# Retention's latent pass: element-wise sums moved from GpSimd to VectorE, and later adaLN products

## The chip, the cores and the metric

The kernel runs on one core of a Trainium2 chip. Five engines share the work and run side by side, each taking its own instructions strictly in order: TensorE (PE: matmuls and transposes), VectorE (DVE), ScalarE (ACT), GpSimd (POOL) and SyncE (SP, which here issues most of the loads). They wait for each other through semaphores. The metric is device time in microseconds (us) of one launch.

## The reference, cut to what matters

Two layers over 512 latent tokens and 256 context tokens of width 1024, all in float32. The first layer mixes tokens by neighbourhood attention and spatial gating, the second by retention; each ends with a gated MLP. The change lies in the second layer's mixer, with eight heads of 128 key columns and 256 value columns:

```python
q, k, v, g = jnp.split(h_lat @ w_in, splits, axis=-1)
q = apply_rope(q.reshape(B, T, H, dk), cos, sin)
k = apply_rope(k.reshape(B, T, H, dk) * dk ** -0.5, cos, sin)
for d in range(2):                       # forward and backward over the tokens
    s_ctx = retention_final_state(rev(kc), rev(vc), lg)
    outs_lat.append(rev(retention_chunked(rev(q), rev(k), rev(v), lg, s_ctx)))
y_lat = retention_output(outs_lat[0] + outs_lat[1], g, gn_g, w_out)

def apply_rope(x, cos, sin):
    x1, x2 = jnp.split(x, 2, axis=-1)
    return jnp.concatenate([x1 * c - x2 * s, x1 * s + x2 * c], axis=-1)
```

So each head needs keys, queries, values and gates of all latent tokens, two decay matrices, and the state that the context tokens leave behind. Beside this, every layer takes shift, scale and gate vectors ("adaLN") from a product of SiLU(c) with a 1024 x 6144 matrix.

## The kernel before, in words

A float32 product is made of three fast products: every operand is split into a high part (ACT writes it) and a low part (DVE writes the difference), and `mm3` adds high x high, high x low and low x high. `split` stands behind every weight and every activation that a matmul reads, so each loaded 128x1024 weight tile costs one ACT and one DVE instruction.

Retention runs in two passes. The **context pass** goes over the eight heads and makes each one's context state: weights `rck`, `rcv`, products into `rkc` and `rvc`, states `stc` (written to memory as `rsd`). In the same loop the adaLN products for later stages are slipped in, one step of a job at a time, by `self.bg(...)`: a step loads two 512 KB tiles (`ar`) on SP's queue and runs four matmuls `ad`, a later step copies the sum (`mr`) and adds the bias row by a DMA that POOL issues, and for a gate a last one makes the product `ag`. The weight tiles of the heads and the `ar` tiles share three buffers named `raw`.

The **latent pass** goes over the heads again. The keys and queries of a head, and then its values and gates, are one 2x2 block product that is worked by a seven-product scheme in the manner of Strassen: instead of eight products there are seven, whose operands are sums of blocks. On the weight side the function `sums` makes four such sums per product, three by GpSimd and one by VectorE, each followed by a split: `a1`, `a2` (weights as loaded), `s2`, `q3`, `q4`, `s3` (sums), `b2`. In the trace the weights of a head h are `rwk`/`rwq` (128x512 halves, for keys and queries) and `rwa1`, `rwa2`, `rwb1`, `rwb2` (128x1024, for values and gates), their split forms `rkq..` and `rvg..`; the products go to the PSUM tiles `Xkq`, `Ykq`, `Zkq` and `Xvg`, `Yvg`, `Zvg`. The results gather in `kp` and `qp` (keys, queries) and `vp`, `rv`, `rg` (values, gates). `rope` turns `kp` and `qp`: ACT copies swapped halves to `sw`, GpSimd multiplies them with `sin`, VectorE multiplies the tile with `cos` and adds both. `decay` makes the decay matrix of a head from two exponentials (`e`): a product and a sum with the identity, both on GpSimd.

`kq_product` calls `after(n)` behind each of its seven products, and `vg_product` likewise; the main loop's `in_kq` and `in_vg` put other work there: the next weights' steps (`step`), the decay, the transposes of the previous head's output (`gated`, tiles `rt`), and one eighth of the previous head's output projection (`o()`: six matmuls `w`, an ACT copy `ryp` and a DMA `yr` that POOL issues). The one wait that the text below speaks of most is that of the seventh product `Xkq<-sar`: it writes PSUM tile X again, so it must wait until DVE's instruction `qp<-qp,Xkq` has read the sixth product from it.

What the program code says is not quite the order on the engines: a scheduler, with an own account of costs, sets each engine's order from the program and its dependencies.

All engine operations pass through one helper, so nearly every instruction of the trace has its line, 64 (63 after the change).

Of the kernel before, what the change touches and what calls it, by code (L numbers as in the profile page):

```python
# [13 lines left out]
ALU = mybir.AluOpType  # L14
# [15 lines left out]
NEG = -1e30  # L30
RB = 32
GF = 2
CTX_BG = 1
ND = 389
EARLY = 2
TWO = ((0, (0, 1), 0, True), (1, (2,), 0, False), (1, (3,), 128, True))
# [35 lines left out]
class Trunk:  # L72
# [1098 lines left out]
    def retention(self, y, final):  # L1171
        S, V, T, G, a = self.S, self.V, self.T, self.G, self.a
        KS = float(np.float32(P) ** np.float32(-0.5))
        with ExitStack() as ctx:
# [6 lines left out]
            sin = rp.tile([P, 512], F32, name="sin", tag="sin")  # L1181
# [31 lines left out]
            def ctx_keys(h):  # L1213
                ps = self.ps(f"rkc{h}", "A")
                self.proj_t(ps[:, :256], hd[h]["wk"], 1)
                if h:
                    kc = rp.tile([P, 256], F32, name=f"kc{h}", tag=("pre0", "pre1")[h % 2], bufs=1)
                else:
                    kc = self.t2k("kc0", shape=(P, 256))
                hd[h]["kc"] = kc  # L1220
                S.activation(kc, ps[:, :256], AF.Copy, scale=KS)
# [65 lines left out]

            def sums(a1, a2, b1, b2, put, both=None):

                add = lambda o, x, y: G.tensor_tensor(out=o, in0=x, in1=y, op=ALU.add)  # L1290
                if both:
                    put("a1", both)
                else:
                    put("a1", a1)
                    yield
                    put("a2", a2)
                add(a1, a1, b1)
                add(b1, b1, b2)
                yield
                put("s2", b1)  # L1300
                V.tensor_tensor(out=b1, in0=a1, in1=b2, op=ALU.add)
                add(a2, a2, b1)
                yield
                put("q3", b1)
                yield
                put("q4", a2)
                yield
                put("s3", a1)
                yield
                put("b2", b2)  # L1310
                yield
# [73 lines left out]
            def decay(h):  # L1385
                d = hd[h]
                e = d["e"] = []
                for i in range(2):
                    t = rp.tile([P, ND], F32, name=f"e{i}{h}", tag=f"e{i}", bufs=1)
                    lg = dec[:, 8 * i + h : 8 * i + h + 1]  # L1390
                    S.activation(t, dist[:, i * ND : i * ND + ND], AF.Exp, scale=lg)
                    e.append(t)
                dl = d["dl"] = e[0][:, 0:384]
                G.tensor_tensor(out=dl, in0=dl, in1=e[1][:, 0:384], op=ALU.mult)
                G.tensor_tensor(out=dl[:, 128:256], in0=dl[:, 128:256], in1=self.ident, op=ALU.add)

            def rope(x, dst, scale, name):

                sw = self.t2k(f"sw{name}")

                def one():
                    for o, i in ((slice(0, 64), slice(64, 128)), (slice(64, 128), slice(0, 64))):
                        S.activation(sw[o], x[i], AF.Copy, scale=scale)
                    G.tensor_tensor(out=sw, in0=sw, in1=sin, op=ALU.mult)
                    V.scalar_tensor_tensor(out=x, in0=x, scalar=scale, in1=cos, op0=ALU.mult, op1=ALU.mult)

                def two():
                    V.tensor_tensor(out=x, in0=x, in1=sw, op=ALU.add)
                    self.split(dst[0], dst[1], x)

                return one, two
# [239 lines left out]
            for h in range(8):  # L1651
                ctx_keys(h)
                if h == 1:
                    self.need(1)
                if h:
                    ctx_states(h - 1)
                ctx_values(h)
                if h < 7:
                    ctx_weights(h + 1)
                else:  # L1660
                    kq = kq_weights(0)
                    next(kq)
                    next(kq)
                if h == 0:
                    self.need(0)
                elif h < 5:
                    next(blocks, None)
                if h == 5:
                    self.load(cos, a["cos"])
                    self.load(sin, a["sin"])  # L1670
                    self.load(gng, a["gn_col"])
                if h == 6:
                    vg = vg_weights(0)
                self.bg(CTX_BG)
            ctx_states(7)
            for _ in kq:
                pass
            out = []

            def o():  # L1680
                if out:
                    out.pop(0)()
# [8 lines left out]
            def step(x):  # L1691
                if x:
                    next(x, None)

            for h in range(8):
                d = hd[h]
                f, later = [], None

                def in_kq(n):
                    if n == 0:  # L1700
                        o()
                        if h in (0, 6, 7):
                            step(vg)
                    elif n == 1:
                        o()
                        if 0 < h < 6:
                            wo.append(w_out(h - 1))
                    elif n == 2:
                        o()
                        decay(h)  # L1710
                    elif n == 3:
                        o()
                        step(vg)
                    elif n == 4:
                        step(vg)
                    elif n == 5:
                        if h:
                            f.extend(gated(h - 1))
                            if h < 6:
                                out.extend(out_steps(h - 1, f, list(wo)))  # L1720
                            else:
                                feats.extend(f)
                    elif n == 6:
                        step(vg)

                def in_vg(n):
                    nonlocal later
                    if n == 0:
                        step(vg)
                        self.bg()  # L1730
                    elif n == 1:
                        step(vg)
                    elif n == 2:
                        step(vg)
                        context(h)
                        self.bg()
                        if h < 7:
                            later = kq_weights(h + 1)
                    elif n == 3:
                        step(vg)  # L1740
                        score(h, 0)
                    elif n == 4:
                        self.bg()
                    elif n == 5:
                        score(h, 1)
                        states(h)
                        within(h, 0)
                        step(later)

                kq_product(h, in_kq)  # L1750
                vg_product(h, in_vg, o)
                if h == 7:
                    self.bg_all()
                    flat = lambda b: [self.blk[b].rearrange("p x k c -> p x (k c)")[:, x] for x in range(2)]
                    at = [flat(("t", 1)), flat(("t", 2)), flat(22), self.at_slot(3, "rwo3"), flat(("t", 3)), self.at_slot(0, "rwo5")]
                    ws = [self.unit(row(10 + i), f"rwo{i}", at[i]) for i in range(4)]
                    for t in toks:
                        y[t] = self.ytile(t, "yr")
                        self.load(y[t], yd[t])
                    sums_ = {(t, n): self.ps(f"wr{t}{n}", "A") for t in toks[:2] for n in range(2)}  # L1760

                    def part(t, n, fs):
                        c, o = self.gcol(t), slice(512 * n, 512 * n + 512)
                        for i in fs:
                            self.mm3(sums_[t, n], [x[:, c] for x in feats[i]], [x[:, o] for x in ws[i]], i == 0, i == 5)
                step(later)
                step(later)
                within(h, 1)
                step(later)
                step(later)  # L1770
                step(later)
                if h < 7:
                    vg = vg_weights(h + 1)
                if h < 5:
                    wo[:] = []
                    wo.append(w_out(h))
                across(h, 0)
                across(h, 1)
                across(h, 2)
                across(h, 3)  # L1780
                norm(h)
# [7 lines left out]
            for t in toks:  # L1789
                for n in range(2):  # L1790
# [3 lines left out]
                    o = slice(512 * n, 512 * n + 512)  # L1794
# [523 lines left out]
```

## Time and profile before

| | |
|---|---|
| median of 3 runs | 1889.61 us (1889.36 to 1892.18) |
| the profiled execution's own time | 1894.07 us |
| its span, first to last instruction | 1892.3 us |
| busy, share of the span | PE 94%, DVE 75%, ACT 59%, POOL 24% |
| context pass of retention, about | 905 to 1044 us of the span |
| latent pass of retention, about | 1044 to 1480 us of the span |
| latent pass alone: PE, DVE, ACT, POOL busy | 406.9, 360.7, 264.8, 184.7 of 436 us |

Matmuls overlap each other, so a PE that is busy is not one at its peak; what can be read directly is where PE sits idle and who ended the wait. An instruction's time is from its start to its end, stalls while it runs included. In the rows, `out<-in` names the tiles written and read, `x8` counts instructions, and `<-` behind an idle time names who ended it.

### The profile page before, as it was taken

The numbers are of one execution on the slowest core, as the hardware profiler recorded it, in microseconds if no ns is written. First come the engines' busy times: TensorE is split into PE (matmuls) and PEld (weight loads), VectorE is DVE, ScalarE is ACT, GpSimd is POOL, SyncE is SP. The second block draws the span as 40 slices with busy tenths as digits, with TensorE's granted clock in tenths as the row PEclk, the third lists the DMA queues.
The fourth block names the chain that finished last, engine by engine and source line by source line (L and its number), as shares of the span: only waits on it lengthen the run. The fifth ranks groups of instructions, "written<-read, shape, count | busy, mean of one in ns | idle before, by whom it ended". The sixth has DMA issues, their size and how long they took to land. (4 is left out here: it accounts for less than half of the span.)

```text
span 1892.3 us, 29833 instructions
## 1 busy us (share of the span) xinstructions
PE 1785.2 (94%) x11240; PEld 1587.8 (84%) x11240; DVE 1424.1 (75%) x2349; ACT 1114.6 (59%) x2038; POOL 454.3 (24%) x533
## 2 busy tenths in 40 slices
PE   6999999999999999998999899999998989999998
PEld 4887677889889899898778788888898789899987
DVE  4543567579787887778876778778889689788887
ACT  4533567466555655555575556666666477576664
POOL 1111211100222222221211334434543100222221
PEclk9999999999999999999999999999999989999999
DMA  7432332324687776776576343665433324777773
GB/s 303 134 103 87 115 106 68 122 80 145 162 184 178 156 164 139 171 149 166 213 228 220 121 150 116 152 163 128 103 93 106 123 91 145 179 199 178 174 182 103
DMA packets 95488, 279.21 MB, mean 148 GB/s; under 512 B 12528, under 2 KB 14064, under 8 KB 95344
## 3 DMA queue, kind: packets, MB, share of 16 engines
q1 hardware_dynamic: 63568, 217.88, 35.2%
q0 software_dynamic: 31200, 59.31, 18.6%
q8 instruction: 88, 1.44, 0.3%
q14 instruction: 56, 0.46, 0.1%
q10 hardware_dynamic: 576, 0.11, 0.0%
HBM read 208.06 MB, written 52.43 MB: 138 GB/s over the span
## 5 line engine op out<-in xcount | busy, mean ns | idle before, releaser
L64 DVE SCALAR_TENSOR_TENSOR cv<-pre,cw,cv 128x769 f32<-128x769 f32 (+1 forms) x176 | 152.7, 880 | 7.7 <-ACT cv L64 6.9
L64 POOL DMA_DIRECT2D yf<-yp x64 | 55.7, 871 | 262.8 <-ACT yp L64 166.0
L64 ACT ACTIVATE cv<-pre,cw 128x770 f32<-128x770 f32 (+1 forms) x88 | 81.0, 923 | 38.9 <-DVE pre L64 37.6
L64 DVE SCALAR_TENSOR_TENSOR acc<-ar,cs,acc 128x512 f32<-128x512 f32 x112 | 81.7, 746 | 27.0 <-DMA ar<-in_adaw 16.1
L64 POOL DMA_DIRECT2D yd<-yp x54 | 46.6, 871 | 193.1 <-ACT yp L64 189.3
L64 POOL DMA_DIRECT2D yd<-ypg x54 | 45.9, 875 | 150.6 <-ACT ypg L64 150.2
L64 ACT COPY yp<-wf 128x512 f32<-128x512 f32 x118 | 67.8, 576 | 18.1 <-PE wf L64 17.9
L64 ACT ACTIVATE pre<-px 128x256 f32<-128x256 f32 (+2 forms) x160 | 54.2, 366 | 38.6 <-PE px L64 38.0
L64 ACT ACTIVATE g<-cv 128x770 fp32r<-128x770 f32 (+1 forms) x44 | 32.4, 737 | 29.4 <-DVE cv L64 29.1
L64 POOL DMA_DIRECT2D yr<-ryp x40 | 32.9, 822 | 58.2 <-ACT ryp L64 50.8
L64 PE MATMUL ad<-ar,c 128*32 128x512 f32 (+1 forms) x320 | 41.5, 530 | 4.6 <-DMA ar<-in_adaw 4.5
L64 PE MATMUL px<-hs,wd 128*128 128x384 f32 x240 | 45.3, 336 | 0.4 <-DVE pre L64 0.4
L64 PEld LDWEIGHTS px<-hs,wd 128*128 128x128 f32 x240 | 42.3, 188 | 2.3 <-DVE pre L64 0.8
L64 ACT ACTIVATE pre<-py 128x384 f32<-128x384 f32 (+1 forms) x40 | 17.4, 435 | 44.9 <-DVE cv L64 27.1
L64 ACT ACTIVATE cv<-cv 128x770 f32<-128x770 f32 (+1 forms) x44 | 32.7, 743 | 15.7 <-DVE cv L64 15.5
L64 POOL TENSOR_TENSOR tm<-slab,mask 128x256 f32<-128x256 f32 (+1 forms) x32 | 25.5, 826 | 65.9 <-DVE sst L64 65.7
L64 DVE TENSOR_TENSOR g<-cv,g 128x770 fp32r<-128x770 f32 (+1 forms) x44 | 36.1, 821 | 6.5 <-ACT g L64 6.1
L64 ACT COPY ryp<-w 128x512 f32<-128x512 f32 x40 | 23.4, 584 | 27.1 <-DMA yr<-ryp 14.9
L64 DVE CUSTOM_DVE_ANT_0 sc<-s,tm 128x256 f32<-128x256 f32 x32 | 13.5, 421 | 33.5 <-PE s L64 24.6
L64 DVE TENSOR_TENSOR pre<-pre,pz 128x256 f32<-128x256 f32 (+1 forms) x60 | 20.9, 371 | 23.2 <-PE pz L64 23.1
L64 ACT ACTIVATE sc<-sc,sst 128x512 f32<-128x512 f32 x32 | 23.2, 726 | 25.3 <-DVE sc L64 23.0
L64 PEld LDWEIGHTS px<-hs 128*128 128x128 f32 x240 | 32.0, 197 | 6.7 <-DVE pre L64 5.5
(2996 smaller groups left out, 7034.1 us busy)
## 6 DMA issues: line engine op xcount, KB each, us to landing
ar<-in_adaw SPq DMA_DIRECT2D x96, 512.0 KB, 4.0
yf<-yp POOLq DMA_DIRECT2D x64, 256.0 KB, 4.2
yd<-yp POOLq DMA_DIRECT2D x54, 256.0 KB, 5.1
yd<-ypg POOLq DMA_DIRECT2D x54, 256.0 KB, 4.7
yr<-ryp POOLq DMA_DIRECT2D x40, 256.0 KB, 4.2
fin<-xd SPq DMA_DIRECT2D x10, 512.0 KB, 4.2
xd<-xd SPq DMA_DIRECT2D x8, 512.0 KB, 3.2
xn<-in_x SPq DMA_DIRECT2D x6, 512.0 KB, 4.7
```

Of the source, the lines that this page charges most:

```text
L64: r = f(*p, **k)
```

## The change

It does five things.

1. In `sums`, all four weight sums run on VectorE (three of them were on GpSimd). Per head these are three 128x512 and three 128x1024 instructions.
2. In `decay`, the product (128x384) and the sum with the identity (128x128) run on VectorE.
3. In `rope`, the product with `sin` (128x512, for keys and for queries) runs on VectorE, behind the product with `cos`.
4. In the context pass the adaLN steps begin at head 3: five steps there instead of eight. The steps run on in the latent pass, three per head as before.
5. One of the eight output-projection pieces of a head moves from behind the fourth key/query product to behind the sixth.

```diff
-CTX_BG = 1
@@ sums
-                add = lambda o, x, y: G.tensor_tensor(out=o, in0=x, in1=y, op=ALU.add)
+                add = lambda o, x, y: V.tensor_tensor(out=o, in0=x, in1=y, op=ALU.add)
...
                 put("s2", b1)
-                V.tensor_tensor(out=b1, in0=a1, in1=b2, op=ALU.add)
+                add(b1, a1, b2)
                 add(a2, a2, b1)
@@ decay
-                G.tensor_tensor(out=dl, in0=dl, in1=e[1][:, 0:384], op=ALU.mult)
-                G.tensor_tensor(out=dl[:, 128:256], in0=dl[:, 128:256], in1=self.ident, op=ALU.add)
+                V.tensor_tensor(out=dl, in0=dl, in1=e[1][:, 0:384], op=ALU.mult)
+                V.tensor_tensor(out=dl[:, 128:256], in0=dl[:, 128:256], in1=self.ident, op=ALU.add)
@@ rope, one()
-                    G.tensor_tensor(out=sw, in0=sw, in1=sin, op=ALU.mult)
                     V.scalar_tensor_tensor(out=x, in0=x, scalar=scale, in1=cos, op0=ALU.mult, op1=ALU.mult)
+                    V.tensor_tensor(out=sw, in0=sw, in1=sin, op=ALU.mult)
@@ the context pass
-                self.bg(CTX_BG)
+                if h > 2:
+                    self.bg()
@@ in_kq
                     elif n == 3:
-                        o()
                         step(vg)
                     elif n == 4:
                         step(vg)
                     elif n == 5:
+                        o()
                         if h:
                             f.extend(gated(h - 1))
```

What this makes of the order on the engines shows at three places.

**VectorE, key/query product of head 3.** Before (`kp`, `qp`: keys and queries in the making; `rvga1`, `rvga2`: first weights of the following value/gate product; `gt`: the previous head's output):

```order
L64 TENSOR_TENSOR kp_11809<-kp_11809,Zkq_11813 128x256
L64 TENSOR_TENSOR rwo21l<-rwo21r,rwo21h 128x1024
L64 TENSOR_TENSOR rvga13l<-rwa13r,rvga13h 128x1024
L64 TENSOR_TENSOR kp_11809<-kp_11809,Ykq_11812 128x256
L64 TENSOR_TENSOR rvga23l<-rwa23r,rvga23h 128x1024
L64 TENSOR_TENSOR qp_11810<-qp_11810,Xkq_11811 128x256
L64 SCALAR_TENSOR_TENSOR kp_11809<-kp_11809,cos 128x512
L64 SCALAR_TENSOR_TENSOR gt_11956<-rt_11957,gng,gt_11955 128x512
```

and now:

```order
L63 TENSOR_TENSOR e_11858<-e_11858,e_11860 128x384
L63 TENSOR_TENSOR e_11858<-e_11858,ident 128x128
L63 TENSOR_TENSOR kp_11781<-kp_11781,Ykq_11784 128x256
L63 TENSOR_TENSOR qp_11782<-qp_11782,Xkq_11783 128x256
L63 SCALAR_TENSOR_TENSOR kp_11781<-kp_11781,cos 128x512
L63 TENSOR_TENSOR swk_11900<-swk_11900,sin 128x512
L63 TENSOR_TENSOR kp_11781<-kp_11781,swk_11900 128x512
L63 TENSOR_TENSOR rvga13l<-rwa13r,rvga13h 128x1024
L63 TENSOR_TENSOR rvga23l<-rwa23r,rvga23h 128x1024
L63 TENSOR_TENSOR rwa13r<-rwa13r,rwb13r 128x1024
L63 SCALAR_TENSOR_TENSOR gt_11928<-rt_11929,gng,gt_11927 128x512
L63 TENSOR_TENSOR rwb13r<-rwb13r,rwb23r 128x1024
```

The two splits `rvga1`, `rvga2` stood ahead of and between the reads of Y and X, and now stand behind the whole turning of the keys; the weight sums stand on this queue behind them. Heads 2, 4 and 5 show the same.

**TensorE, the same product.** Before, the piece of the output projection (`w`) stands between the fourth product (`Xkq<-h1c`) and the fifth (`Ykq<-h1c`):

```order
L64 MATMUL Xkq_11811<-h1c,rkq13l 128x256
L64 MATMUL w_11905<-rwo10h,gt_11314 128x512
L64 MATMUL w_11905<-rwo10l,gt_11314 128x512
L64 MATMUL w_11905<-rwo10h,gt_11315 128x512
L64 MATMUL w_11905<-rwo11h,gt_11314 128x512
L64 MATMUL w_11905<-rwo11l,gt_11314 128x512
L64 MATMUL w_11905<-rwo11h,gt_11315 128x512
L64 MATMUL Ykq_11812<-h1c,rkq23h 128x256 x2
```

and now, behind the sixth (`Xkq<-rt3b`) and ahead of the transposes and the seventh:

```order
L63 MATMUL Xkq_11783<-rt3b,rkq23l 128x256
L63 MATMUL w_11918<-rwo10h,gt_11286 128x512
L63 MATMUL w_11918<-rwo10l,gt_11286 128x512
L63 MATMUL w_11918<-rwo10h,gt_11287 128x512
L63 MATMUL w_11918<-rwo11h,gt_11286 128x512
L63 MATMUL w_11918<-rwo11l,gt_11286 128x512
L63 MATMUL w_11918<-rwo11h,gt_11287 128x512
L63 MATMUL rt_11929<-ident,rg_11331 128x128 x4
L63 MATMUL rt_11936<-ident,rg_11331 128x128 x4
L63 MATMUL Xkq_11783<-sar_9413 128x256 x12
```

Between the sixth product, whose result DVE must take from X, and the seventh, which writes X, six more matmuls have come to stand. Heads 2 to 6 show this.

**SyncE, context pass.** Before, the first adaLN tiles (`ar`) stand ahead of the weights of head 2 (`rck2`):

```order
L64 DMA rcv11r<-in_ret_vg 128x1024
L64 DMA ar_8967<-in_adaw 128x1024
L64 DMA xd_111<-fin 128x1024
L64 DMA ar_8971<-in_adaw 128x1024
L64 DMA dist<-in_dist 128x778
L64 DMA cos<-in_cos 128x512
L64 DMA sin<-in_sin 128x512
L64 DMA rck2r<-in_ret_qk 128x1024
```

and now `rck2` stands behind `rcv11`, and the first `ar` ahead of `rck5`:

```order
L63 DMA rcv41r<-in_ret_vg 128x1024
L63 DMA rsd_8791<-sc_9324 128x512
L63 DMA ar_9423<-in_adaw 128x1024
L63 DMA ar_9427<-in_adaw 128x1024
L63 DMA rck5r<-in_ret_qk 128x1024
L63 DMA rcv50r<-in_ret_vg 128x1024
L63 DMA rcv51r<-in_ret_vg 128x1024
```

Of the 24 `ar` loads of this stage, eight stood ahead of the latent pass's first key weights (`rwk0`) before, and four do now; the others stand behind it.

## The prediction

> **What bounds the kernel now.** I read the page's first part, then the stretch of the latent pass alone, then who makes TensorE wait there, and last the instructions around the longest of these waits.
>
> ```profile
> PE 1785.2 (94%) x11240; PEld 1587.8 (84%) x11240; DVE 1424.1 (75%) x2349; ACT 1114.6 (59%) x2038; POOL 454.3 (24%) x533
> core 0: 1892.3 us, clock 0.982
> 905.00:1044.00 139.00, 126.84 (x875) 109.83 (x873) 100.28 (x157) 89.09 (x189) 23.08 (x33) 0.98 0.64 213
> 1044.00:1480.00 436.00, 406.93 (x2940) 375.56 (x2941) 360.68 (x568) 264.78 (x419) 184.65 (x151) 0.98 0.46 128
> ```
>
> The last two rows are the context pass and the latent pass; after the length stand the busy times of PE, PE's weight loads, DVE, ACT and POOL. TensorE is the bound, and it is idle for 436.0 - 406.9 = 29.1 us of the latent pass. No matmul is added or removed, so the change can only gain or lose idle time of TensorE: at most about 29 us here, and 139.0 - 126.8 = 12.2 us in the context pass. Who ends these waits (total, times, longest), the first eight rows for the latent pass, the last for the context pass:
>
> ```profile
> PE Xkq L64 <- DVE qp L64: 10.4, 5, 2.4
> PE kn L64 <- DVE kp L64: 4.2, 3, 1.4
> PE stl L64 <- DVE rv L64: 4.0, 5, 1.1
> PE stl L64 <- ACT rv L64: 2.3, 1, 2.3
> PE Xkq L64 <- ACT kp L64: 2.3, 2, 2.1
> PE rt L64 <- DVE rg L64: 2.2, 1, 2.2
> PE Xvg L64 <- ACT vp L64: 1.5, 3, 0.7
> PE rx L64 <- DVE of L64: 1.1, 1, 1.1
> PE ad L64 <- DMA ar<-in_adaw: 4.5, 2, 2.7
> ```
>
> Nearly all of it is VectorE coming late. Head 3 shows why (start, duration, engine; the third row is the same wait in head 7):
>
> ```profile
> 1221.55 1.04 PE L64 MATMUL rt<-ident,rg 128*128 128x128 f32 x8
> 1224.85 1.70 PE L64 MATMUL Xkq<-sar 128*128 128x256 f32 x12 [2.26 <-DVE qp L64]
> 1440.63 1.70 PE L64 MATMUL Xkq<-sar 128*128 128x256 f32 x12 [1.36 <-DVE qp L64]
> 1220.43 0.41 DVE L64 TENSOR_TENSOR kp<-kp,Ykq 128x256 f32<-128x256 f32 x1
> 1220.81 3.65 DVE L64 TENSOR_TENSOR rvga23l<-rwa23r,rvga23h 128x1024 fp32r<-128x1024 f32 x1
> 1224.38 0.41 DVE L64 TENSOR_TENSOR qp<-qp,Xkq 128x256 f32<-128x256 f32 x1
> 1224.71 2.54 DVE L64 SCALAR_TENSOR_TENSOR kp<-kp,cos 128x512 f32<-128x512 f32 x1
> 1227.18 1.40 DVE L64 SCALAR_TENSOR_TENSOR gt<-rt,gng,gt 128x512 fp32r<-128x512 f32 x2
> 1220.68 2.69 POOL L64 TENSOR_TENSOR rwa13r<-rwa13r,rwb13r 128x1024 f32<-128x1024 f32 x1
> 1223.45 3.27 POOL L64 TENSOR_TENSOR rwb13r<-rwb13r,rwb23r 128x1024 f32<-128x1024 f32 x1
> ```
>
> DVE's split `rvga23l` lasts 3.65 us: it begins 0.13 us behind GpSimd's sum `rwa13r` and ends 1.1 us after it, as if it had run only then. Behind it stands `qp<-qp,Xkq`, which TensorE needs to write X again: 2.26 us idle. `kp<-kp,cos` meets the next GpSimd sum in the same way, while `gt`, which reads PSUM and one SBUF tile beside its scalars, keeps 0.7 us each next to GpSimd's work. So where both engines read SBUF pairs they take turns, and GpSimd's slow instruction is paid by DVE.
>
> **The change part by part.** Prices on both engines (min/median/max in ns, or busy us and mean ns):
>
> ```profile
> L64 POOL TENSOR_TENSOR rwb13r<-rwb13r,rwb23r x1: 3265/3265/3265, 1223.4 to 1223.4; 128x1024 f32<-128x1024 f32 x1
> L64 DVE TENSOR_TENSOR rwb13r<-rwa13r,rwb23r x1: 1211/1211/1211, 1232.5 to 1232.5; 128x1024 f32<-128x1024 f32 x1
> L64 POOL TENSOR_TENSOR rwk3r<-rwk3r,rwq3r x2: 1411/1536/1660, 1192.2 to 1197.2; 128x512 f32<-128x512 f32 x2
> L64 DVE TENSOR_TENSOR rwq3r<-rwk3r,rwq3r x1: 693/693/693, 1196.4 to 1196.4; 128x512 f32<-128x512 f32 x1
> L64 DVE SCALAR_TENSOR_TENSOR kp<-kp,cos x8: 677/2545/2787, 1056.1 to 1441.6; 128x512 f32<-128x512 f32 x8
> L64 DVE SCALAR_TENSOR_TENSOR qp<-qp,cos x8: 679/1768/1781, 1063.0 to 1446.3; 128x512 f32<-128x512 f32 x8
> L64 DVE TENSOR_TENSOR rg<-of,rg 128x256 f32<-128x256 f32 x29 | 10.9, 414 | 0.0
> L64 POOL TENSOR_TENSOR swk<-swk,sin 128x512 f32<-128x512 f32 x8 | 15.3, 1908 | 7.8 <-ACT swk L64 7.8
> L64 POOL TENSOR_TENSOR e<-e,e 128x384 f32<-128x384 f32 x8 | 8.2, 1024 | 21.4 <-ACT e L64 20.9
> ```
>
> What DVE takes on, per head: three sums of 128x1024 at 1.21 (3.63), three of 128x512 at 0.69 (2.08), two sin products at 0.68 (1.36), the decay's two at about 0.55 and 0.21, estimates between and below the 414 ns of 256 columns and the 693 of 512. That is 7.8 us a head, 62.7 us over eight heads. What DVE is relieved of: `rvga2` 3.65 - 1.21 = 2.44, `kp<-kp,cos` 2.55 - 0.68 = 1.87, `qp<-qp,cos` 1.77 - 0.68 = 1.09: 5.4 us a head from three instructions; over eight heads the two `cos` rows alone give, at their medians, 23.7 us. With the rest of the stretched instructions I estimate some 50 us. So DVE's busy time hardly changes (360.7 + 63 - 50 = 374 of 436 us), and it no longer stalls at the moments that TensorE waits for. GpSimd loses work that nothing then waits for; its remaining yr DMAs and norm scalars start sooner.
>
> Now the waits, one by one, read against the new order.
>
> *Xkq <- DVE qp, 10.4 us in five.* Four of the five are heads 2 to 5, 9.0 us, the fifth head 7's 1.36. In heads 2 to 5 the splits that stood ahead now stand behind, and six matmuls `w` stand between X's sixth product and its seventh: some 1.4 us, an estimate from the 1.70 of twelve matmuls of half their width, the last one's run-out left off. By head 3's rows the sixth product ended where the transposes begin, at 1221.55; with the `w` piece behind it instead of ahead, it ends at about 1220.2. DVE has read it by 1220.8, and the transposes end at 1222.6 as before, now followed without a break. The 9.0 us fall away. In head 7 one sum of 1.21 us is put ahead of other work, and a split stands no longer between the reads: I take 0.5. Bounds 6 and 10.4.
>
> *What is late next in these heads.* The splits `rvga1`, `rvga2` wait behind four instructions of 0.68 (cos, sin, sum) and 0.41: from 1220.8 three times 0.68 and 1.21 end `rvga1` at about 1224.1, and `Xvg` wants it when the seventh product has been issued, 1222.6 + 1.5 = 1224.1. That is level. I charge 0.3 us for each of five heads, 1.5 us; bounds 0 and 6 (one split of 1.21 late each time).
>
> *stl <- rv, 6.3 us in six.* The values wait on `rv`, behind weight splits that waited for GpSimd's sums. The sums now stand on DVE ahead of `vp<-vp,Yvg` (two at 0.69), but no hand-over to GpSimd remains. I take half, 3.2; bounds -3 (two sums late in each head, less the slack of the product between) and 6.3.
>
> *kn <- kp, 4.2 us, heads 0, 6 and 7.* There DVE has sums of 1.21 ahead of the keys' turning, in place of a sin product of 1.9 on GpSimd. I take 0; bounds -4 and 4.2.
>
> *rt <- rg, 2.2 us, head 1.* The norm's scalars stood on GpSimd's queue behind two weight sums of 1024 columns, which leave: gain 2.0, bounds 0 and 2.2. *Xkq <- ACT kp, 2.3*: ACT stood in front of a weight tile that came late because its buffer was held by splits behind GpSimd's sums: 1.0, bounds 0 and 2.3. *Xvg <- vp, 1.5*: 0.5. *rx* stays.
>
> Together for the latent pass: 9.5 - 1.5 + 3.2 + 0 + 2.0 + 1.0 + 0.5 = 14.7 us.
>
> *The adaLN steps.* TensorE waits 4.5 us in two places for `ar` tiles. The first, 2.7 us, goes; but the first steps now stand ahead of head 4's and 5's keys behind weight loads in the same three buffers, and may wait there as they did (the second wait, 1.8 us, was ahead of head 5's keys). SP's queue brings head 2's weights sooner, for which no wait is listed. One step, four matmuls, moves into the latent pass: its time moves, it is not added. I take 1.3 us; bounds -2 and 4.5. The moved piece `o()` of each head also moves a copy on ACT and a DMA on POOL's queue; ACT waits for these DMAs today, as the first row shows, and they are released sooner:
>
> ```profile
> ACT ryp L64 <- DMA yr<-ryp: 14.9, 10, 2.9
> DVE of L64 <- POOL rrr L64: 15.7, 16, 1.9
> ```
>
> The sum is 14.7 + 1.3 = 16.0 us. The profiled execution took 1894.07 us (span 1892.3, so 1.8 outside it); less 16.0 it would take 1878.1. It lies 4.5 us above the median of the runs shown, 1889.61, so for the median I expect 1873.6.
>
> **The rivals.** *The waits move.* Everything stands in order on DVE, and 7.8 us of new work a head lies among what TensorE waits for: `rvga1` late by a whole split (6 in place of 1.5), the values late by the two sums (no gain at `stl`), one 1.2 us loss more at `kn` in three heads, nothing from the adaLN steps. That is 16.0 - 4.5 - 3.2 - 3.6 - 1.3 = 3.4 us gained: about 1886. For it speaks that all of it leans on an order that is level to a few tenths of a microsecond; against it that DVE idles 75 of 436 us.
>
> *More falls away.* If DVE without stalls is ahead everywhere, the 23.2 us of the first five rows of waits go, the 2.2 of `rt` and the 4.5 of the adaLN: 29.9 us, 1860. Against it: heads 0, 6 and 7 put sums of 1.21 us ahead of the meets.
>
> *DVE becomes the bound, slower.* If the stretched instructions are long for another reason than GpSimd's sums, DVE keeps its 360.7 us and gets 62.7 more, 423 of 436, with its 75 us of waiting for others mostly still to pay. If half of those remain, the pass is 423 + 38 = 461 us, 25 us longer: 1915. It decides from a `kp<-kp,cos` that still takes over 2 us. Against it stands the row of this instruction, 677 at its least and 2545 in the middle, and `rvga23l`'s end right behind GpSimd's. The Trainium skill, Perfetto Trace Analysis (Optimizing Scalar/DVE Operations), would have a saturated DVE hand work to other engines, even GPSIMD, which this change undoes; it adds that the two share a read port, so that it might not help. By the first half the outcome is this rival's; this case's trace bears out the second half, with 3.65 us for a split that alone takes 1.21.
>
> *The change doesn't do what it says* only in the adaLN: the steps may wait in their new places as in the old, which is inside the bounds above.
>
> **How the numbers follow.** The forecast has a chance of 0.58, with a range of its own of 1867 to 1881; moved waits 0.20 (1881 to 1889); more falls away 0.13 (1857 to 1867); DVE the bound 0.09. Leaving out the last and the far half of the third, the range is 1862 to 1887. A difference under 0.2% (3.8 us) can't be told from none. Faster by more: all of the first and third and half of the second, 0.81; within: 0.10; slower: 0.09.
>
> **What the changed profile would show.** In heads 2 to 5 no wait of `Xkq<-sar` for `qp` over 0.3 us; `kp<-kp,cos` and `qp<-qp,cos` at 0.68 us in all heads; `rvga2` at 1.2; DVE busy within 15 us of 360.7 in the latent pass; PE idle there some 14 us instead of 29. It would be wrong if `Xvg` waits for `rvga1` by a microsecond in each head, if `stl` waits longer than 6.3 us in all, or if DVE's instructions are still stretched with GpSimd idle. A lower granted clock in the latent pass (0.98 now) would hide the gain.

## The result and the profile after

The changed kernel takes 1855.7 us (median of 4 runs, 1854.6 to 1857.06), the kernel before 1889.93 us beside it (1889.36 to 1892.18): a ratio of 0.9817, 95% interval 0.98 to 0.9834. The gain is 34.2 us. The forecast was 1873.6 us with a gain of 16.0, the range 1862 to 1887: the direction is right, the size under half, and the time lies below the range. One execution of the decay kernel and one of a filled kernel, each slower than all others of its kernel, are left out of the figures below.

First the page's busy line, and the context and latent pass by windows of both kernels, cut at the same matmuls (length; busy us of PE, PE's weight loads, DVE, ACT, POOL; granted clock; DMA). After:

```profile
PE 1774.4 (96%) x11240; PEld 1582.9 (85%) x11240; DVE 1423.8 (77%) x2429; ACT 1113.2 (60%) x2038; POOL 315.4 (17%) x453
904.00:1033.10 129.10, 121.88 (x865) 108.09 (x863) 100.96 (x164) 89.24 (x189) 15.51 (x26) 1.00 0.63 213
1033.10:1440.00 406.90, 399.36 (x2952) 369.91 (x2951) 359.11 (x640) 262.99 (x418) 52.45 (x77) 1.00 0.51 141
```

Before:

```profile
905.00:1044.30 139.30, 126.84 (x875) 109.83 (x873) 100.45 (x158) 89.39 (x190) 23.08 (x33) 0.98 0.64 213
1044.30:1480.00 435.70, 406.93 (x2940) 375.56 (x2941) 360.51 (x567) 264.48 (x418) 184.65 (x151) 0.98 0.46 128
```

Two things fall. TensorE's idle time goes from 139.30 - 126.84 = 12.5 to 7.2 us in the context pass and from 28.8 to 7.5 us in the latent pass: 26.5 us together. And TensorE's busy time falls as well, by 5.0 and 7.6 us, though its 11240 matmuls are the same. The last column but two says where to look: the granted clock is 0.98 before and 1.00 after. Cut finer, the kernel before shows where its clock was low:

```profile
959.90:1000.20 40.30, 36.70 (x265) 32.12 (x263) 32.40 (x53) 29.49 (x60) 3.11 (x4) 0.92 0.75 238
1044.30:1095.00 50.70, 45.80 (x341) 42.48 (x342) 35.12 (x46) 28.36 (x45) 20.18 (x11) 0.93 0.35 121
1095.00:1150.00 55.00, 52.60 (x373) 47.90 (x372) 44.84 (x77) 31.55 (x51) 17.80 (x18) 0.94 0.44 140
1150.00:1207.00 57.00, 55.09 (x392) 50.34 (x391) 46.66 (x74) 35.69 (x57) 26.20 (x23) 0.97 0.51 152
```

In the traces the granted clock is either 1.00 or 0.50, the latter in stretches of 3.4 us or a small multiple of it; the text calls them half clock. Length times missing clock gives 40.3 x 0.08 + 50.7 x 0.07 + 55.0 x 0.06 + 57.0 x 0.03 = 11.8 us lost before. After, one such window is left in these passes, head 7's with 53.45 us at 0.97, 1.6 us. So of the 39.0 us by which the two passes are shorter in this pair of profiles (575.0 to 536.0), 26.5 are idle time, 10.2 are clock, and 2.3 are not assigned. (The pair is 39.5 us apart, the medians 34.2: the profiled execution of before was a long one. Against the second profile of before, taken below, the two passes are 34.1 us shorter: 22.7 of idle time, again 10.2 of half clock, and 1.2 not assigned. So some 4 us of the idle time come and go with the execution.)

The waits that are left in the latent pass, by who ends them (total, times, longest), and the one adaLN wait that is left in the context pass:

```profile
PE Xvg L63 <- DVE kp L63: 2.7, 2, 2.5
PE Ykq L63 <- ACT qp L63: 1.5, 1, 1.5
PE stl L63 <- DVE rv L63: 1.1, 3, 0.4
PE kn L63 <- DVE kp L63: 1.0, 1, 1.0
PE Xkq L63 <- ACT kp L63: 0.6, 1, 0.6
PE ad L63 <- DMA ar<-in_adaw: 0.4, 1, 0.4
```

`Xkq` no longer waits for `qp` at all. Head 3, the place of the prediction's rows, reads (start, duration, engine):

```profile
1194.57 1.03 PE L63 MATMUL rt<-ident,rg 128*128 128x128 f32 x8
1195.36 1.68 PE L63 MATMUL Xkq<-sar 128*128 128x256 f32 x12
1193.38 0.42 DVE L63 TENSOR_TENSOR qp<-qp,Xkq 128x256 f32<-128x256 f32 x1 [0.95 <-PE Xkq L63]
1193.77 0.69 DVE L63 SCALAR_TENSOR_TENSOR kp<-kp,cos 128x512 f32<-128x512 f32 x1
1196.85 1.22 DVE L63 TENSOR_TENSOR rvga23l<-rwa23r,rvga23h 128x1024 fp32r<-128x1024 f32 x1
L63 DVE SCALAR_TENSOR_TENSOR kp<-kp,cos x8: 684/692/694, 1045.5 to 1402.4; 128x512 f32<-128x512 f32 x8
```

Now VectorE waits for TensorE (0.95 us), the split takes 1.22 us in place of 3.65, and `cos` takes 0.69 us in every head, where the middle one had taken 2.5.

### The profile page after: what moved, and what is told of

The parts are those of the page before. It is cut to its first block, busy times and chain, and to the rows that moved or that the text cites. A ratio compares the mean times of both kernels' runs of the same rounds, so it can differ in the third digit from the quotient of the medians.

```text
span 1852.8 us, 29765 instructions
## 1 busy us (share of the span) xinstructions
PE 1774.4 (96%) x11240; PEld 1582.9 (85%) x11240; DVE 1423.8 (77%) x2429; ACT 1113.2 (60%) x2038; POOL 315.4 (17%) x453
## 5 line engine op out<-in xcount | busy, mean ns | idle before, releaser
L63 DVE SCALAR_TENSOR_TENSOR acc<-ar,cs,acc 128x512 f32<-128x512 f32 x112 | 81.8, 748 | 27.9 <-DMA ar<-in_adaw 16.7
L63 ACT ACTIVATE cv<-cv 128x770 f32<-128x770 f32 (+1 forms) x44 | 32.7, 743 | 15.7 <-DVE cv L63 15.5
L63 PE MATMUL px<-hs 128*128 128x256 f32 x240 | 33.6, 291 | 5.4 <-DVE pre L63 5.4
L63 DVE TENSOR_TENSOR cv<-cv 128x770 f32<-128x770 f32 (+1 forms) x44 | 36.2, 824 | 1.0
```

Source lines behind the costliest of these rows:

```text
L63: r = f(*p, **k)
```

## The experiments

Each row is one kernel. The gain is against the median of the kernel before in the same group of runs, which varied from 1885.8 to 1890.9 us between groups; the ratio carries its 95% interval. "Clock" is the span times the missing share of the granted clock, the median over a kernel's runs (32.1 us over 86 runs of before).

| edit | median us | gain us | ratio | clock us |
|---|---|---|---|---|
| before again | 1888.0 | -0.9 | 1.0005 (0.998 to 1.0031) | 34.9 |
| all three VectorE parts | 1860.5 | 26.6 | 0.984 (0.9802 to 0.9879) | 27.0 |
| only the sums | 1865.9 | 20.6 | 0.9884 (0.9845 to 0.9923) | 26.1 |
| only the sin products | 1880.6 | 5.3 | 0.9975 (0.9954 to 0.9996) | 30.1 |
| only the decay | 1884.7 | 6.1 | 0.9967 (0.9941 to 0.9993) | 31.1 |
| only the adaLN start | 1877.8 | 9.4 | 0.9932 (0.9907 to 0.9957) | 27.2 |
| only the output piece | 1899.1 | -8.2 | 1.0056 (1.0035 to 1.0076) | 36.0 |
| whole change, piece put back | 1855.2 | 32.0 | 0.9804 (0.9771 to 0.9837) | 25.0 |
| whole change, second group of runs | 1853.9 | 32.6 | 0.9823 (0.9788 to 0.9859) | 24.1 |
| whole change, third group of runs | 1860.0 | 28.5 | 0.9842 (0.9817 to 0.9867) | 26.0 |

**The kernel before, once more.** No edit. The theory to be tested: a wait of TensorE costs more than its length, because half clock follows some of the waits (the clock theory). The rival: GpSimd's traffic had slowed the matmuls (the neighbour theory).

> The kernel before, unchanged, looked at a second time. Clock theory: a wait of TensorE costs its own length and, where much of one short window of the granted clock is idle, some microseconds at half clock behind it; which of the waits of 1.9 to 2.7 us do so depends on where they fall against those windows, so a second execution shows the same waits (each to 0.1 us, 29 us of idle in the latent pass) but half clock behind other ones of them, two to six in the context and latent passes. Neighbour theory (TensorE's matmuls were slowed by GpSimd's traffic): PE busy in the latent pass is 406.9 us again to 1 us, and the lower clock stands at the same four places. Time 1889 to 1894 us under both.

Nearly all waits came back (`Xkq` for `qp` 10.2 us in five, `kn` 4.2; the one for `rg` in head 1 did not, and the adaLN wait was 1.9 us long instead of 2.7). Half clock stood behind seven of them instead of four: one of the four was gone, three came again, and those of heads 3, 4, 5 and 7 were new. TensorE's busy time in the latent pass, 406.6 us, was that of the first profile, as the neighbour theory had it; the places were not. The windows around the wait of head 3, in the second execution (two stretches of 3.4 us, the one with the wait and the next):

```profile
1215.40:1218.80 3.40, 1.49 (x12) 1.50 (x13) 3.40 (x3) 0.43 (x1) 3.32 (x2) 0.99 0.26 46
1218.80:1222.20 3.40, 3.40 (x18) 3.40 (x17) 3.40 (x5) 2.49 (x4) 2.06 (x2) 0.50 0.01 2
```

and in the first:

```profile
1223.10:1226.50 3.40, 1.65 (x13) 1.65 (x14) 3.40 (x3) 0.35 (x1) 3.32 (x2) 1.00 0.10 18
1226.50:1229.90 3.40, 3.40 (x33) 3.23 (x35) 3.40 (x5) 2.63 (x5) 1.92 (x2) 1.00 0.01 2
```

The same wait of the same kernel, the same GpSimd work beside it (3.32 us): once 18 matmuls are begun in the next 3.4 us, once 33. In this second execution 1.91 us of the window were idle, in the first 1.75; the rest of the wait lay in the window before. The neighbour theory cannot have that, with the same neighbour. The Trainium skill, TensorE: Matmul & The Clock Gate (What's actually happening), has TensorE's clock halved after an idle window of about 3.4 us of a free-running timer. The trace agrees on the length (half clock comes in stretches of 3.4, 6.8 and 10.2 us) and on chance deciding which wait is hit; but here a window that was idle for 1.9 of its 3.4 us was enough. All twenty profiles bear this out when they are cut on the clock's own grid of 3.41 us: of 189 windows at full clock with 1.9 us or more idle, half clock followed 188; of 148 with 1.45 to 1.9 us, 55; of some 10 200 with less, one.

What it costs shows over many executions: in 86 runs of the kernel before (spans 1875.8 to 1901.6 us) span and lost clock go together with a correlation of 0.71 and a slope of 0.96 us per us lost; the 23 runs with a clock of 0.981 or less have a mean span of 1891.3, the 14 with 0.985 or more one of 1881.2. In the mean, before loses 33.1 us to the clock and the changed kernel 25.2 (15 runs). At that slope **some 7.5 of the 31.1 us between the two mean spans are clock** (the clock is listed to 0.001, 1.9 us, for each run). This is worked out from executions that differ by chance; that taking lost clock away gives the time back is tried further below.

**The parts alone.** All of VectorE's parts without adaLN and output piece; then each alone.

```diff
 # vector_only = before with:            # ada_only = before with:
 sums, decay, rope: G.tensor_tensor      -                self.bg(CTX_BG)
   -> V.tensor_tensor, sin behind cos    +                if h > 2: self.bg()
 # o_back = the whole change, but        # o_only = before with:
 n == 3: o(); step(vg)                   n == 3: step(vg)
 n == 5: (no o())                        n == 5: o(); gated(...)
```

> Weight sums, sin and decay products on VectorE; adaLN steps and the moved output piece as before. Clock theory: nearly all idle of the latent pass goes, 29 to some 9 us, and with it most of the half clock there (8.5 us lost in the profiled execution of before): 26 to 30 us faster than before, about 1862; the adaLN wait of 2.7 us in the context pass stays, with its half clock in some executions. The prediction's own sum for these parts: 14.7 us, 1875. Neighbour theory: also about 1862, but the PE time of the latent pass falls to 399 us whatever the clock row shows.

> Only the weight sums on VectorE; sin and decay products on GpSimd, adaLN and the output piece as before. Theory: the five long qp waits were made by the splits stretched next to GpSimd's sums of 2.4 to 3.3 us, so most of the gain is here: the qp waits of heads 2 to 5 go (9 us) with stl and their half clock, 15 to 22 us faster, about 1868. Rival: the sin products (1.9 us on GpSimd next to cos on VectorE, two a head) stretch VectorE as much; then under 12 us, 1877 or more.

> Only the sin products on VectorE; sums and decay on GpSimd. With the sums alone 20.6 us were gained of the 26 to 28 of all vector parts. If gains add: 4 to 8 us, about 1881. Rival: the sums still stretch cos and the splits, VectorE now has 0.68 more twice a head ahead of the meets: no gain, 1885 to 1890.

> The kernel before with the decay's two products on VectorE alone. The parts alone were 20.6 us (sums) and 5 us (sin) faster, all three 26 to 28 us: if gains add, 0 to 3 us here, about 1885. Rival: GpSimd's queue is shorter by 1.5 us a head ahead of the norm's scalars, for which TensorE waits in head 1 (2.2 us): 3 to 5 us.

> Only the adaLN steps of the context pass begin at head 3; the rest as before. Clock theory: both adaLN waits go (4.5 us) and with the longer one its half clock (3.4 us lost in the profiled execution, less on average): 5 to 8 us faster, about 1883, GpSimd's work being all still there. The prediction's sum: 1.3 us (1888). Neighbour theory: at most the 4.5 us of waits, and PE busy in the context pass stays at 126 to 127 us.

The vector parts came out as the clock theory had them, 26.6 us, of which the sums alone give 20.6; sums, sin and decay alone add up to 32.0, within what such intervals allow. The sums' expectation of where the gain lies was only half met: with them alone a wait of `Xkq` for `qp` of 0.5 to 1.9 us is left in six heads (7.1 us in all), and goes when the sin products move as well. The sin products gave what was expected of them; the decay gave more than its 0 to 3 us and the rival's 3 to 5, with an interval of the ratio that reaches from 1 to 11 us. AdaLN gave 9.4 us, more than the 5 to 8 expected and seven times the prediction's 1.3. Not both of its waits went, as expected: waits for `ar` of 2.3 us in three places are left of 4.5. By windows the idle time of its context pass fell by 3.3 us, half clock there was gone (0.98 to 1.00), and ten matmuls moved on to the latent pass, which got no longer for it (430.7 us against 435.7 and 432.5 in the two profiles of before). The expectation left out that last part; the interval of the ratio reaches from 8 to 18 us.

**The moved output piece.** The prediction's largest term (9.0 us in heads 2 to 5) gave it the cover for the read of X.

> The whole change, but the moved output piece stands before the fourth keys-and-queries product again. By the prediction this piece gave 6 matmuls of cover for the read of X ahead of the seventh product: without it 1 to 1.4 us of wait in each of heads 2 to 5, 4 to 6 us slower than the whole change, about 1860 to 1862, more if the half clock follows. Rival: with DVE unstalled the read is early anyway, and the whole change's 1855.7 us stays within 1.5 us.

> The kernel before with the moved output piece alone; GpSimd's work and the adaLN steps as they were. The prediction gave this piece some 1.4 us of cover ahead of the seventh product in each of heads 2 to 5. If it covers also while VectorE is stretched: qp waits of heads 2 to 5 down from 9 to some 3.5 us, 4 to 8 us faster than before with the half clock behind them, about 1881. Rival (what is late is VectorE's split, not the read of X, so that moving the matmuls only moves the wait): the waits of heads 2 to 5 stay over 7 us in all or turn up ahead of the next product, within 2 us of before.

Both theories that gave the piece a value fell. Put back, it changes nothing (1855.2 us): the seventh product hardly waits then either (0.7 us once in the latent pass). But the scheduler sets it behind the first values product there, so this run alone does not show that no cover is needed. Its rows in head 3, transposes first:

```profile
1194.04 1.03 PE L64 MATMUL rt<-ident,rg 128*128 128x128 f32 x8
1197.77 0.60 PE L64 MATMUL at<-ident,mr 128*128 128x128 f32 x4
1198.32 1.70 PE L64 MATMUL Xkq<-sar 128*128 128x256 f32 x12
```

The changed kernel's rows above say more: VectorE has read X at 1193.80, while the piece still runs (the transposes begin at 1194.57). Without the piece's 1.4 us the seventh product would begin at about 1194.0, an estimate from these rows, still 0.2 us behind the read. Alone, with GpSimd's sums still there, the piece makes the kernel 8.2 us slower. The waits for `qp` do go, but turn up elsewhere, and VectorE's `cos` of the queries is caught worse than before:

```profile
PE stl L64 <- ACT rv L64: 9.1, 3, 4.3
PE stl L64 <- DVE rv L64: 5.6, 6, 1.2
PE Yvg L64 <- DVE rvgs25l L64: 2.3, 1, 2.3
PE Yvg L64 <- DVE rvgs24l L64: 2.2, 1, 2.2
PE Xkq L64 <- DVE qp L64: 1.4, 1, 1.4
1221.86 4.55 DVE L64 SCALAR_TENSOR_TENSOR qp<-qp,cos 128x512 f32<-128x512 f32 x1
```

**Is it GpSimd's reading, or waiting for its results?** All runs so far removed both. The first try put products on GpSimd that nobody waits for beside every sum of the changed kernel:

```diff
 def add(o, x, y):
     V.tensor_tensor(out=o, in0=x, in1=y, op=ALU.add)
+    for _ in range(o.shape[1] // 128):
+        G.tensor_tensor(out=self.ones, in0=ones, in1=ones, op=ALU.mult)
```

> The changed kernel with products of a small constant tile with itself (128x128, read and written on GpSimd) put beside every weight sum, 48 a head; nobody reads or waits for them, and the order on VectorE, ScalarE and TensorE is that of the changed kernel. Collision theory (VectorE's instructions were stretched by GpSimd's reads themselves): next to them VectorE's two-input instructions are long again (128x1024 over 1.6 us instead of 1.21, cos over 0.9 instead of 0.68), VectorE's busy time in the latent pass rises by 20 us or more, waits of TensorE come back: 1860 to 1880. Rival (VectorE was late because it waited for results of GpSimd, not because of its reads): nothing changes, 1854 to 1857.

It answered another question: 1997.6 us. As the products depend on nothing, the scheduler moved nearly all of them far ahead, into FFN 1, where GpSimd's queue issues the DMAs that ScalarE's output tiles wait for; the latent pass itself was as fast as ever. PE's waits there (600 to 1010 us) and the group of the products:

```profile
PE wf L63 <- ACT yp L63: 46.7, 5, 25.2
PE wf L63 <- ACT ypg L63: 39.0, 7, 11.9
PE px L63 <- ACT pre L63: 35.2, 4, 14.0
L63 POOL TENSOR_TENSOR ones<-ones 128x128 fp32r<-128x128 f32 x382 | 214.5, 562 | 27.9
```

The second try ties them to each head's decay, whose second exponential is no longer read by then:

```diff
+def spin(h, n):
+    x = hd[h]["e"][1][:, 0:384]
+    for _ in range(n):
+        G.tensor_tensor(out=x, in0=hd[h]["dl"], in1=x, op=ALU.mult)
 ... # spin(h, 3) behind decay and behind the first three values products
```

> The changed kernel with twelve products of 128x384 on GpSimd behind each head's decay (some 12 us a head), written over a part of the decay tile that is no longer read; no other engine waits for them but ScalarE's next exp of that tile, a head later, and the order on VectorE, ScalarE, TensorE and SyncE is that of the changed kernel. Collision theory: VectorE's instructions next to them are stretched again (cos well over 0.68 us, a split of 128x1024 well over 1.21), 20 us or more of VectorE's time in the latent pass; TensorE's waits for qp, kp and rv come back: 1865 to 1885. Rival (VectorE had waited for GpSimd's results, and its durations do not depend on what GpSimd reads): durations stay within 0.1 us, 1853 to 1858.

1903.0 us, ratio 1.0068 (1.0041 to 1.0095): slower than the kernel before, with every engine but GpSimd in the order of the changed kernel. Head 3's rows, and the latent pass as a whole, cut at the same matmuls as above:

```profile
1212.84 2.02 DVE L63 TENSOR_TENSOR rvga23l<-rwa23r,rvga23h 128x1024 fp32r<-128x1024 f32 x1
1216.73 0.74 DVE L63 SCALAR_TENSOR_TENSOR gt<-rt,gng,gt 128x512 fp32r<-128x512 f32 x1
1220.11 1.50 DVE L63 SCALAR_TENSOR_TENSOR qp<-qp,cos 128x512 f32<-128x512 f32 x1
1224.69 1.21 DVE L63 TENSOR_TENSOR rwb13r<-rwa13r,rwb23r 128x1024 f32<-128x1024 f32 x1
1213.85 8.63 POOL L63 TENSOR_TENSOR e<-e,e 128x384 f32<-128x384 f32 x5
1032.80:1489.10 456.30, 415.35 (x2953) 383.17 (x2952) 407.45 (x640) 264.84 (x418) 180.38 (x161) 0.96 0.46 126
```

While GpSimd's products run (to 1222.5) a split takes 2.02 us and a `cos` 1.50; behind them the same work takes 1.21, and `gt`, which reads PSUM, keeps its 0.74 throughout. The whole pass: VectorE 407 us busy in place of 359, TensorE idle for 41 us in place of 7.5, its clock 0.96, and 49 us more in all. That is above the 20 us and the 1865 to 1885 expected. Waiting for GpSimd's results does not explain it: VectorE's waits for the norm's scalars `rrr`, the only ones of VectorE or ScalarE in this pass that GpSimd ends, are those of the changed kernel (this run's row, then the changed kernel's; in the kernel before 15.7 us in 16):

```profile
DVE of L63 <- POOL rrr L63: 9.3, 14, 1.3
DVE of L63 <- POOL rrr L63: 9.2, 14, 1.3
```

So the collision is shown, and waiting for results is not needed for it. Nothing says that TensorE's matmuls themselves are slowed: 456.3 x 0.04 = 18 us of clock cover the 16 by which PE's busy time is above that of the changed kernel. GpSimd's own products suffer too: 8.63 us for five here, 1.7 each, and 1.34 in the middle of all 96, where this form took 1.02 us in the kernel before.

**Filling waits with matmuls.** If half clock follows idle, unread matmuls in a wait should save it without touching the wait.

```diff
 # fill_before (into Y, 16) and fill_before2 (into Z, 14): before, heads 2 to 5
+for _ in range(16): T.matmul(Y, self.ones, self.blk[11][:, 0, 0, :], start=True, stop=True)
 prod_t(X, w["b2"], ("t", 4), "onto")
 # fill_tail (30 and 22) and fill_tail2 = fill_tail3 (20 and 22): the changed kernel, FFN 2's start
+for _ in range(20): T.matmul(idle, self.ones, self.blk[11][:, 0, 0, :], start=True, stop=True)
 self.need(1)
+for _ in range(22): T.matmul(idle, ...)
 # fill_more: also 16 ahead of head 7's values, 10 behind need(1) in FFN 1
```

> The kernel before with 16 unread matmuls (some 1.9 us) ahead of the seventh keys-and-queries product in heads 2 to 5, where TensorE waits 1.9 to 2.6 us for VectorE; no wait is removed, GpSimd's sums stay. Clock theory: half clock no longer follows these four waits (two profiles of before show it behind one and behind four of them, 1.7 us lost each); 2 to 6 us faster than before, the qp waits together with the added matmuls 9 to 10 us as ever. Neighbour theory: no change, or slower where the added matmuls overrun the wait.

> The kernel before with 14 unread matmuls ahead of the seventh product in heads 2 to 5, now into the tile of the second product, so that the tiles of the values product keep their turn (the first try made it wait 1.4 us a head for VectorE's reads of the transposes). Clock theory: half clock no longer follows these four waits, 2 to 6 us faster than before, about 1882. Rival: the clock lost falls but the time does not, since the work behind the wait is bound by VectorE's queue there anyway: within 2 us of before.

Both miss on time: 1895.6 and 1894.3 us, ratios 1.0037 (1.0009 to 1.0065) and 1.0055 (1.0034 to 1.0076), though the clock lost fell as expected, 33.9 to 29.4 and 32.0 to 28.4 us. The added matmuls moved the order and the PSUM tiles' turns around them; in the first a new wait of 1.4 us a head (`Xvg` for `gt`, 5.7 us) took the place. They say nothing clean on the price.

> The changed kernel, unchanged, beside the others of this call for comparison. Clock theory: 1854 to 1857 us, and half clock behind the waits that are left (the 2.5 us ahead of head 7's values product, the 4.1 and 2.8 us at the end of the retention), some 25 us lost by the clock in all against some 35 in the kernel before.

> The changed kernel with 52 unread matmuls in the two last waits of the retention's end (4.1 and 2.8 us, no other work). The waits themselves stay. Clock theory: the three windows at half clock from 1482.7 on (10.2 us, PE busy 7.1 of them) go, and the some 7 us of work in them run in about half the time: 2.5 to 3.5 us faster than the changed kernel, about 1852. Neighbour theory, or if the half clock comes by chance: no gain, 0 to 1 us slower for the added matmuls.

> The changed kernel with 20 and 22 unread matmuls in the two last waits of the retention's end; the order on all other engines is that of the changed kernel (with 30 and 22 ScalarE's order had changed and put a weight split ahead of what TensorE waits for). Clock theory: half clock behind these waits mostly goes, 2 to 3.5 us faster than the changed kernel's 1853.9, about 1851. Rival: the stretch behind the waits is bound by ScalarE and VectorE, which build its operands, so that a slow TensorE costs nothing there: 1853 to 1855.

> The changed kernel, for comparison with the two below on the same chip: 1852 to 1857 us, 24 to 25 us lost by the clock.

> The changed kernel with the 42 unread matmuls in the two last waits of the retention, once more (1847.7 against 1853.9 of the changed kernel in another call). Clock theory: 3 to 6 us faster than the changed kernel beside it, with 3 to 5 us less lost by the clock. Rival: the difference was one of calls, and it is within 1.5 us.

> As the one before, with 16 unread matmuls in the 2.5 us wait of head 7 and 10 in the 1.8 us wait at the first blocks of FFN 1; the order on the other engines is that of the changed kernel. Clock theory: half clock behind these two waits goes as well (1.7 and 3.4 us lost in the profile of the changed kernel): another 2 to 4 us, about 1845. Rival: VectorE and ScalarE bound the work behind these waits, 0 to 1 us.

The changed kernel came out at 1853.9 us in the first group, `fill_tail` beside it at 1857.2: it had changed ScalarE's order, and missed. The later three leave the order of all other engines as it is. The tail's window at half clock in the changed kernel:

```profile
1482.70:1492.93 10.23, 7.13 (x31) 6.26 (x30) 9.00 (x15) 6.89 (x13) 1.12 (x2) 0.50 0.47 131
```

and the same place with the 42 matmuls:

```profile
1475.90:1486.10 10.20, 9.38 (x72) 8.71 (x73) 9.10 (x16) 7.29 (x15) 1.12 (x2) 1.00 0.48 131
```

Times: `fill_tail2` 1847.7 us; in one group of runs the changed kernel 1860.0, `fill_tail3` 1854.3 and `fill_more` 1852.9, clock lost 26.0, 19.5 and 16.7 us. In the profile of `fill_tail3` two stretches of 3.4 us at half clock are left near this place, and `fill_more` misses its 1845: in its profile head 7's wait for `kp` turns up at `kn` instead (2.3 us), with half clock behind it. Their ratios to before, 0.9842, 0.9823 and 0.9813, have overlapping intervals (0.9794 to 0.9833 for the last). Over all groups the 13 filled runs have a mean span of 1850.2 us and lose 18.8 to the clock, the 15 of the changed kernel 1854.5 and 25.2: some 4 us of time for 6 us of clock. Filled waits look faster than the changed kernel; a single comparison does not separate them.

## Why the prediction was right in sign and wrong in size

**"GpSimd's slow instruction is paid by DVE": right**, and shown by `gpsimd_spin`. VectorE's price was nearly right: busy 359.1 us where 360.7 was the old figure and 374 the estimate. The 62.7 us of new work are paid by stretching that goes, which by this sum is some 64 us and not the 50 estimated.

**"The change can only gain or lose idle time of TensorE: at most about 29 us here": the step that failed.** TensorE's time also depends on its clock, and the clock on the waits: 10.2 us in the pair of profiles, 7.8 less lost in the mean of runs, none in the sum. The row for it was quoted: 0.98. It was read as a mean and kept as something that "would hide the gain", when it stood for 11.8 us in four windows, each behind a wait of 1.9 to 2.7 us (`ad`, `stl`, `rt`, `Xkq`) that the sum was already removing in whole or in half.

**The terms of the sum: too small as a whole**, 16.0 us against 26.5 of idle time. One by one, measured in the one pair of profiles:

| term | predicted gain | measured |
|---|---|---|
| `Xkq` for `qp` (10.4 us) | 9.5 | 10.4, none left |
| `Xvg` for `rvga1`, new | -1.5 | no such wait; for `kp`, mostly head 7, -2.4 |
| `stl` for `rv` (6.3) | 3.2 | 5.2 |
| `kn` for `kp` (4.2) | 0 | 3.2 |
| `rt` for `rg` (2.2) | 2.0 | 2.2 |
| `Xkq` for ACT's `kp` (2.3) | 1.0 | 1.7, with a new one of `Ykq` for `qp`, -1.5 |
| `Xvg` for `vp` (1.5) | 0.5 | 1.5 |
| adaLN (4.5) | 1.3 | 4.1 |
| `rx` and a `stc` (2.1) | 0 | 2.1 |

(Both columns add up: 16.0 and 26.5.) The largest shortfalls are adaLN (2.8 us), `kn` (3.2) and `stl` (2.0). The halved VectorE terms share a mistake, as far as the rows tell: each put VectorE's new instructions ahead of what TensorE waits for, and did not count that the stretched ones ahead of *them* get shorter by as much. With its work equal and no stalls at random places, VectorE was early everywhere but in head 7. The bounds had it (10.4, 6.3, 4.2, 4.5); the chosen values did not. The rival "more falls away", 29.9 us, comes nearest to the idle time, and its 1860 us nearest to the measured time; it was given 0.13, and even it lacked the clock.

**"With the `w` piece behind it instead of ahead": a wrong reason for a right term.** By head 3's rows the 9.0 us came from VectorE being on time, with 0.2 us to spare without the piece; that the term came out was in this part luck. The piece gives nothing with the rest of the change, and costs 8 us without it, where the rival "the waits move" is what happened.

**AdaLN: "may wait there as they did"** did not hold: one wait of 0.4 us is left.

**Not decided:** how the 2.3 us of the pair's difference that are neither idle nor clock come about, how much time a lost microsecond of clock costs (0.96 us by the executions of before, some 0.7 by the filled kernels), and how much of the adaLN part's 9.4 us is its own and how much the clock of those runs.

## What to carry to other kernels

Where TensorE's granted clock is below 1 in a stage, cut the stage into windows until the low ones stand alone and look at the wait in front of each: beside its own length such a wait can cost 1.7 us for each window of 3.4 us at half clock behind it (one or two in these passes, three at the retention's end), and removing it can give both. Before you count GpSimd's share of element-wise work as free, compare the shortest and the middle duration of VectorE's instructions of one form; if they are far apart next to GpSimd's work, that difference is GpSimd's price. And a reordering that helps a stalled engine need not help an unstalled one: test it alone and with the rest.

## What was not expected of the hardware

A window idle for 1.9 of 3.4 us is enough for half clock in the next one or two windows. In head 3 1.75 us was not, and in one case (1335.7 to 1339.1 us of the first profile, 1.92 idle) nothing followed either; elsewhere 1.75 us was enough, so the limit is a band of about 1.45 to 1.9 us. The same wait of 2.3 to 2.4 us had nothing behind it in one execution and 3.4 us at half clock in the next, and executions of one kernel differ by up to 25.8 us, about half of whose variance goes with the lost clock (correlation 0.71). And two-way collisions are paid by both: 12 products of 128x384 a head on GpSimd lengthened VectorE's work by 48 us in eight heads, and took 1.34 us in the middle themselves instead of 1.02.
